# Last chunk of both MLPs in a trunk kernel: from four plain quadrants to the seven products, in an order that completes the first half of the tokens two products early

## The chip, the cores and the metric

The kernel runs on one core of a Trainium2 chip. The metric is the device time of one execution, in microseconds (us); the median of three runs is the time of a kernel. The engines are TensorE (PE, with its weight loads as PEld), VectorE (DVE), ScalarE (ACT), GpSimd (POOL) and SyncE (SP), which here only starts DMAs.

## The reference, cut to what matters

A trunk of two layers works on x, 512 tokens by 1024 features in float32. Layer 0 mixes tokens by latent attention, layer 1 by an mLSTM. After each mixer comes an MLP with squared ReLU, and these two MLPs are what the change touches:

```python
def sqrelu_mlp(h, w1, w2):
    return jnp.square(jax.nn.relu(h @ w1)) @ w2

for i in range(DEPTH):                       # DEPTH = 2
    ...
    x = x + y.astype(x.dtype)                # y: the token mixer
    x = x + sqrelu_mlp(rms_norm(x, norm_ffn[i]), ffn_w1[i], ffn_w2[i])
```

w1 is 1024 by 4096 and w2 is 4096 by 1024.

## The kernel before

**Stages.** The program runs four stages in turn: the attention mixer, MLP 0, the mLSTM mixer, MLP 1. Both MLPs are the same function `ffn` with `last` false or true. The residual x lies in SBUF as eight tiles `xs[t, f]` of 128 tokens by 512 features (t = 0 to 3, f = 0 or 1).

**Numbers.** Every float32 operand is split into a high and a low part. A weight tile of 128x1024 is cast by ACT (`wh`), and DVE subtracts that from the original (`wl<-tw,wh`, or `zw` where the pair lies in a borrowed z tile; a hidden tile gives `hh` and `hl`). A product is then three matmuls: high by high, high by low, low by high. All of the names in the rows are of this kind: `tw` is a raw tile of w2, `wr` another raw weight, `z` a hidden tile, `tp` and `mm` are PSUM banks from two pools (four and three buffers).

**Chunks.** The 4096 hidden features go in NC = 8 chunks of 512. The first matrix is worked through in units ("F", i), i = 0 to 31, 24 matmuls each, four to a chunk. The second is multiplied by Winograd's form of Strassen's seven products, units ("P", c, n): a 2 by 2 block product in seven block products rather than eight. Each unit is 12 matmuls: two token tiles (one PSUM bank each) of six. The table `PROD` gives for n = 0 to 6 the left side, the right side, the chain of banks, and the quadrant (th, f) of x that the bank is added into: 0 A11·b11, chain a, (0,0); 1 S1·t1, chain b, (1,1); 2 S2·t2, a, (0,1); 3 S4·b22, b, (0,1); 4 S3·t3, a, (1,1); 5 A12·b21, c, (0,0); 6 A22·t4, a, (1,0). A chain's two banks gather several products, and after each product two DVE instructions (`y_add`, written y{c}{n} below; in rows `x<-tp,r,x`) add the banks into x. S1 to S4 are sums of hidden blocks, four POOL instructions of 128x256; t1 to t4 are sums of weight blocks, one POOL instruction of 128x1024 each. t2 is written over b11 and t4 over t1.

**The last chunk before.** Chunk 7 is plain: `l_split` splits b11, b21, b12, b22 as they are, and `l_mm` works four quadrants, each of two token tiles of 12 matmuls, 96 in all, without sums. After quadrant (1,0) the transposes of the finished token half stand between the matmuls (`half`).

**What follows.** In MLP 1 `half` is `out`: four PE transposes into an `mm` bank, a copy to a `t` tile of 128x512 by ACT or DVE, and one DMA to the output; there are two `t` tiles. In MLP 0 it is `nxt.half`, which transposes and splits x as the mLSTM's input (`xg`); what is left of it (`nxt.tail`) runs behind the first block of the mLSTM's matmuls.

**Order.** DVE's and PE's instructions of `ffn` are kept in the order of the code (`idve`, `ipe`); ACT's and POOL's in `ffn` and all others are placed by a scheduler. The list `units` sets the order of units; `ahead` splits weights two units early. Around the end of an MLP it is, with Pcn for ("P", c, n): P60 F29 P61 F30 P62 P63 F31 P64 P65 P66, and then the quadrants.

Of the kernel before, what the change touches and what calls it, by code (L numbers as in the profile page):

```python
# [17 lines left out]
F32R = mybir.dt.float32r  # L18
# [43 lines left out]
def trunk(ctx: ExitStack, tc, a, yT, dbg=None):  # L62
# [661 lines left out]
    def ffn(fp, layer, last):  # L724
# [28 lines left out]
        def f_post(ps, i):  # L753

            c, p = i // 4, i % 4 // 2
            plain = c == NC - 1
            if i % 2 == 0:
                zs[c, p] = fp.tile([P, 8, 256], F32, tag="z", bufs=3, name=nm("z"))
            z = zs[c, p]
            t_ = tmp()  # L760
            iact.activation(t_, ps, AF.Relu)
            iact.activation(z[:, 1:3] if i % 2 else z[:, 0:4:3] if plain else z[:, 0:8:7],
                            t_.rearrange("p (h e) -> p h e", h=2), AF.Square)
            if i % 2 == 0:
                return
            hi = fp.tile([P, 7, 256], F32R, tag="hh", bufs=4, name=nm("hh"))
            lo = fp.tile([P, 7, 256], F32R, tag="hl", bufs=4, name=nm("hl"))
            hs[c, p] = hi, lo

            def split(b):  # L770
                iact.copy(hi[:, b], z[:, b])
                idve.tensor_sub(lo[:, b], z[:, b], hi.bitcast(F32)[:, b])

            if plain:
                later.append([s_now[0] + 1, lambda: split(slice(0, 4))])
                return
            ipool.tensor_add(z[:, S1], z[:, A21], z[:, A22])
            ipool.tensor_sub(z[:, S2], z[:, S1], z[:, A11])
            ipool.tensor_sub(z[:, S3], z[:, A11], z[:, A21])
            ipool.tensor_sub(z[:, S4], z[:, A12], z[:, S2])  # L780
            later.append([s_now[0] + 1, lambda: split(slice(0, 3))])
            later.append([s_now[0] + 2, lambda: split(slice(3, 7))])
# [16 lines left out]
                tw[c, n] = b(to)  # L799

        def s_split(c, n):
            ws["P", c, n] = split_w(tw[c, PROD[n][1]], D, iact, idve)

        def s_mm(c, n):
            lhs, _, chain, (th, f) = PROD[n]
            wh, wl = ws.pop(("P", c, n))
            new = n in (0, 1, 5)
            if n < 2:
                bank[chain] = [ps_tp(), ps_tp()]
            for t in range(2):  # L810
                ps = bank["b" if chain == "c" else chain][t]
                for p in range(2):
                    lh, ll = (x[:, lhs, t * P:(t + 1) * P] for x in hs[c, p])
                    rh, rl = (x[:, p * 512:(p + 1) * 512] for x in (wh, wl))
                    skip = not new
                    ipe.matmul(ps, lhsT=lh, rhs=rh, start=new and p == 0, stop=False, skip_group_check=skip)
                    ipe.matmul(ps, lhsT=lh, rhs=rl, start=False, stop=False, skip_group_check=skip)
                    ipe.matmul(ps, lhsT=ll, rhs=rh, start=False, stop=p == 1, skip_group_check=skip)

            def post():  # L820
                for t in range(2):
                    y_add(2 * th + t, f, bank["b" if chain == "c" else chain][t])
# [6 lines left out]
        def l_split(n, roomy):  # L829

            to = None
            if roomy:
                z = fp.tile([P, 2, D], F32R, tag="z", bufs=3, name=nm("zw"))
                to = z[:, 0], z[:, 1]
            ws["L", n] = split_w(tw[NC - 1, n], D, iact, idve, to=to)

        def l_mm(th, f, t, part=slice(0, 12)):
            ps = bank["L", f][t]
            todo = []
            for h in range(2):  # L840
                wh, wl = ws["L", f"b{h + 1}{f + 1}"]
                for p in range(2):
                    lh, ll = (x[:, ((A11, A12), (3, A22))[th][h], t * P:(t + 1) * P] for x in hs[NC - 1, p])
                    rh, rl = (x[:, p * 512:(p + 1) * 512] for x in (wh, wl))
                    todo += [(lh, rh), (lh, rl), (ll, rh)]
            for n in range(12)[part]:
                ipe.matmul(ps, lhsT=todo[n][0], rhs=todo[n][1], start=n == 0, stop=n == 11)
# [28 lines left out]

# [30 lines left out]
        s_sum(0, "t1")  # L907
        s_load(0, ("b21", "b22"))
        s_sum(0, "t3")
        for s_ in range(2, len(units)):  # L910
            u = units[s_]
            if u[0] == "F":
                ps = ps_mm()
                f_mm(ps, u[1])
                ws.pop(u)
            else:
                post = s_mm(u[1], u[2])
            ahead(s_)
            s_now[0] = s_
            while later and later[0][0] <= s_:  # L920
                later.pop(0)[1]()
            if u[0] == "F":
                f_post(ps, u[1])
                if s_ < 5:
                    norm.square(s_ - 1, 0)
                    norm.square(s_ - 1, 1)
                    if s_ == 4:
                        idve.reciprocal(r2, norm.stat())
            else:
                post()  # L930
# [9 lines left out]
                if c == NC - 2 and k > 3:  # L940
                    if k == 4:
                        l_split("b11", False)
                    elif k == 5:
                        l_split("b21", True)
                    else:
                        l_split("b12", True)
# [9 lines left out]
        for n, (th, f) in enumerate(((0, 0), (0, 1), (1, 0), (1, 1))):  # L956
            bank["L", f] = [ps_tp(), ps_tp()]
            for t in range(2):
                if last and n == 3 and t == 1:
                    l_mm(th, f, t, slice(0, 8))  # L960
                    out(4, (2,))
                    l_mm(th, f, t, slice(8, 12))
                else:
                    l_mm(th, f, t)
                if n == 0 and t == 0:
                    l_split("b22", True)
                y_add(2 * th + t, f, bank["L", f][t])
                if n == 2:
                    half(0, ((0, 2), (4, 6))[t])
                if n == 3 and t == 0:  # L970
                    half(1, (0, 2))
                if not last and n < 2:
                    nxt.square(t, f)
                if not last and n == 3:
                    nxt.square(2 + t, 0)
# [8 lines left out]
    def mlstm(lp):  # L984
# [62 lines left out]
        for h in range(MH):  # L1047
# [7 lines left out]
            for t in range(NB):  # L1055
# [216 lines left out]
```

## Time and profile before

| what | before |
|---|---|
| three runs | 1138.22, 1137.02, 1136.86 us; median 1137.02 |
| profiled execution | 1137.65 us; its span, first to last instruction, 1135.8 us |
| mean granted TensorE clock | 0.998 of full speed |
| busy shares | PE 98%, PEld 84%, DVE 73%, ACT 49%, POOL 40% |

The span is the time between the first and the last instruction in the trace; the device time holds 1.85 us more around it. Shares are means over the whole span. The stretch in which the change lies is the last 40 us or so of each MLP: about 548 to 585 us (MLP 0) and 1097 us to the end (MLP 1).

### The profile page before, as it was taken

Reading aid. Unit: us, or ns where it says so; the run is one execution under the profiler, and the core shown is the slowest. Engines: PE = TensorE matmul, PEld = TensorE weight load, DVE = VectorE, ACT = ScalarE, POOL = GpSimd, SP = SyncE. Lnnn points to the kernel's source line nnn. Section 1 sums busy time; section 2 is a strip of 40 time slices with the busy share of each in tenths; the row PEclk is TensorE's granted clock in tenths of the full one; section 3 lists DMA queues with packets and bytes.
Section 4 is the critical chain, followed back from the end, with each engine's and each line's share of the span. In section 5 each row is a group of like instructions: output and inputs, shape, how many; then the busy total and the mean of one; then the engine's idle time right before and its main releaser. Section 6 shows DMA issues by size and latency. Waiting matters only on the chain.

```text
span 1135.8 us, 15650 instructions
## 1 busy us (share of the span) xinstructions
PE 1113.4 (98%) x5802; PEld 949.7 (84%) x5802; DVE 824.1 (73%) x1284; ACT 553.0 (49%) x969; POOL 455.1 (40%) x453
## 2 busy tenths in 40 slices
PE   7899999999999999999999999999999999999998
PEld 7889988888888888888898898888888888888886
DVE  7689997456798788778766465454588779779863
ACT  4468876336544444445455333332655444444451
POOL 6667785207356347335011011010537437436500
PEclk9999999999999999999999999999999999999999
DMA  6301021433432333343203222232333343333212
GB/s 204 115 25 47 20 76 38 134 102 118 130 102 76 119 111 90 96 130 93 76 23 106 78 61 88 75 94 82 140 111 93 93 130 93 93 111 108 60 56 74
DMA packets 32428, 104.27 MB, mean 92 GB/s; under 512 B 3424, under 2 KB 6752, under 8 KB 32352
## 3 DMA queue, kind: packets, MB, share of 16 engines
q1 hardware_dynamic: 32352, 103.27, 29.7%
q8 instruction: 46, 0.75, 0.3%
q14 instruction: 30, 0.25, 0.1%
HBM read 101.16 MB, written 2.10 MB: 91 GB/s over the span
## 4 chain that ended last, share of the span: by engine, by line
PE 93%; DVE 3%; POOL 2%; ACT 1%; issue 1%; DMA 0%; SPq 0%; ACTq 0%; POOLq 0%; DVEq 0%
PE mm L80 39%; PE tp L80 38%; PE mm L174 4%; PE mm L176 4%; PE mm L175 4%; PE po L80 3%; PE tp L176 1%; PE tp L175 1%; PE tp L174 1%; DVE wl L80 1%; ACT t L80 1%; DVE x L80 1%; POOL x L80 0%; POOL scr L80 0%; DMA x<-in_xT 0%
## 5 line engine op out<-in xcount | busy, mean ns | idle before, releaser
L80 PE MATMUL mm<-xg,wh 128*128 128x512 f32 (+1 forms) x1088 | 319.2, 377 | 0.0
L80 POOL TENSOR_TENSOR z<-z 128x256 f32<-128x256 f32 x112 | 129.4, 1175 | 320.4 <-ACT z L80 318.2
L80 PEld LDWEIGHTS mm<-xg,wh 128*128 128x128 f32 x1088 | 200.2, 188 | 37.3
L80 DVE TENSOR_TENSOR wl<-tw,wh 128x1024 fp32r<-128x1024 f32 x100 | 172.7, 1727 | 74.8 <-ACT wh L80 74.8
L80 PE MATMUL mm<-xg,wl 128*128 128x512 f32 (+1 forms) x544 | 206.4, 379 | 0.0
L80 POOL TENSOR_TENSOR tw<-tw,tw 128x1024 f32<-128x1024 f32 x56 | 160.1, 2867 | 34.7 <-issue 29.2
L80 PE MATMUL tp<-wh,hl 128*128 128x512 f32 x408 | 159.0, 390 | 1.3 <-DVE hl L80 1.3
L80 DVE TENSOR_TENSOR wl<-wr,wh 128x1024 fp32r<-128x1024 f32 (+1 forms) x72 | 120.0, 1667 | 55.0 <-ACT wh L80 55.0
L80 DVE SCALAR_TENSOR_TENSOR x<-tp,r,x 128x512 f32<-128x512 f32 (+1 forms) x215 | 149.8, 734 | 13.6 <-PE tp L80 13.5
L80 PE MATMUL tp<-wh,hh 128*128 128x512 f32 x408 | 159.1, 390 | 0.0
L80 PE MATMUL tp<-wl,hh 128*128 128x512 f32 x408 | 158.8, 389 | 0.0
L80 ACT ACTIVATE t<-mm 128x512 f32<-128x512 f32 (+3 forms) x97 | 54.3, 560 | 203.9 <-PE mm L80 194.8
L80 PEld LDWEIGHTS mm<-xg,wl 128*128 128x128 f32 x544 | 102.4, 188 | 22.9 <-DVE wl L80 4.5
L80 ACT CAST wh<-tw 128x1024 fp32r<-128x1024 f32 x100 | 104.7, 1047 | 34.4 <-PE tp L80 26.5
L80 ACT CAST wh<-wr 128x1024 fp32r<-128x1024 f32 (+1 forms) x74 | 78.9, 1067 | 32.1 <-PE tp L80 27.7
L80 PEld LDWEIGHTS tp<-wh,hl 128*128 128x128 f32 x408 | 76.6, 188 | 18.0 <-DVE hl L80 2.1
L80 PEld LDWEIGHTS tp<-wh,hh 128*128 128x128 f32 x408 | 76.6, 188 | 16.5 <-ACT zw L80 0.8
L80 PEld LDWEIGHTS tp<-wl,hh 128*128 128x128 f32 x408 | 76.6, 188 | 15.8
L164 DVE TENSOR_TENSOR wl<-wr,wh 128x1024 fp32r<-128x1024 f32 (+2 forms) x43 | 51.4, 1196 | 44.4 <-ACT wh L160 44.3
L80 ACT CAST hh<-z 128x1024 fp32r<-128x1024 f32 (+1 forms) x60 | 57.0, 949 | 53.4 <-POOL z L80 53.4
L80 DVE TENSOR_TENSOR hl<-z,hh 128x1024 fp32r<-128x1024 f32 (+1 forms) x60 | 82.9, 1382 | 0.0
L160 ACT CAST wh<-wr 128x1024 fp32r<-128x1024 f32 (+2 forms) x43 | 42.8, 995 | 77.1 <-PE mm L175 27.9
(275 smaller groups left out, 2065.3 us busy)
## 6 DMA issues: line engine op xcount, KB each, us to landing
wr<-in_w SPq DMA_DIRECT2D x64, 512.0 KB, 3.6
tw<-in_w SPq DMA_DIRECT2D x64, 512.0 KB, 3.6
wr<-in_w_qkv SPq DMA_DIRECT2D x8, 640.0 KB, 4.1
wr<-in_w_oa SPq DMA_DIRECT2D x8, 512.0 KB, 3.7
wr<-in_w_mo SPq DMA_DIRECT2D x8, 512.0 KB, 3.5
wr<-in_w_ob SPq DMA_DIRECT2D x8, 512.0 KB, 3.5
wr<-in_w_v SPq DMA_DIRECT2D x6, 512.0 KB, 3.8
wr<-in_w_z SPq DMA_DIRECT2D x8, 336.0 KB, 4.5
```

The lines of the kernel that those rows point to most:

```text
L80: return lambda *args, **kw: tc.keep_in_program_order(f(*args, **kw)) if self.on else f(*args, **kw)
L160: act.copy(hi[:, :n], raw[:, :n])
L164: dve.tensor_sub(lo[:, :n], raw[:, :n], hi[:, :n].bitcast(F32))
L174: pe.matmul(out, lhsT=lh, rhs=rh, start=start, stop=False)
L175: pe.matmul(out, lhsT=lh, rhs=rl, start=False, stop=False)
L176: pe.matmul(out, lhsT=ll, rhs=rh, start=False, stop=stop)
```

## The change

Chunk 7 of both MLPs goes by the seven products, 84 matmuls, in the order 0, 5, 1, 2, 3, 4, 6. The sums S1 to S4 and t1 to t4 are now made for chunk 7 as for the others. Product 5 (chain c) gets two `mm` banks of its own, where in other chunks it uses chain b's. Products 4 and 6 are worked by single token tiles (`ts`), with the transposes of the first token half between them, since quadrants (0,0) and (0,1) are complete after product 3. Their weights' splits go to z tiles. In MLP 1 the eight output copies are in the order out(0), out(2), out(4), out(6) for the first half and 4, 6 and the two pieces of 0 for the second; in MLP 0 parts 0 and 2 of the second half go into `nxt.tail`.

```diff
@@ f_post
-            plain = c == NC - 1
...
-            if plain:
-                later.append([s_now[0] + 1, lambda: split(slice(0, 4))])
-                return
             ipool.tensor_add(z[:, S1], z[:, A21], z[:, A22])
...
@@ s_split
+            to = None
+            if c == NC - 1 and n in (4, 6):
+                z = fp.tile([P, 2, D], F32R, tag="z", bufs=3, name=nm("zw"))
+                to = z[:, 0], z[:, 1]
+            ws["P", c, n] = split_w(tw[c, PROD[n][1]], D, iact, idve, to=to)
@@ s_mm
-        def s_mm(c, n):
+        def s_mm(c, n, ts=(0, 1)):
...
+            if ts[0] == 0:
+                if n < 2:
+                    bank[chain] = [ps_tp(), ps_tp()]
+                elif n == 5:
+                    bank["c"] = bank["b"] if c < NC - 1 else [ps_mm(), ps_mm()]
...
@@ units
-        for c in range(NC - 1):
-            for k in range(7):
+        for c in range(NC):
+            for k in range(7) if c < NC - 1 else (0, 5, 1, 2, 3):
                 units.append(("P", c, k))
...
+        units += [("P", NC - 1, 4), ("P", NC - 1, 6)]
@@ loop
-                elif k == 5 and c < NC - 2:
+                if k == (5 if c < NC - 2 else 4):
                     s_sum(c + 1, "t1")
-                elif k == 6 and c < NC - 2:
+                elif k == (6 if c < NC - 2 else 5):
                     s_sum(c + 1, "t3")
@@ tail
+        s_mm(C, 4, (0,))()
+        half(0, (0,))
+        s_mm(C, 4, (1,))()
+        half(0, (2, 4, 6))
+        s_mm(C, 6, (0,))()
+        half(1, (4, 6))
         if last:
-            out(4, (3,))
+            post = s_mm(C, 6, (1,))
+            out(0, (2,))
+            post()
         else:
-            nxt.tail = [lambda m=m: nxt.half(1, m, ps_tp) for m in (4, 6)]
+            s_mm(C, 6, (1,))()
...
+        if last:
+            out(0, (3,))
+        else:
+            nxt.tail = [lambda m=m: nxt.half(1, m, ps_tp) for m in (0, 2)]
```

What this does to the order on POOL at the end of MLP 1 is shown first; these are POOL's last sums before the change, hidden sums of chunk 6 and then t1 to t4 of chunk 6 (the digits behind a name only number buffers).

```order
L80 TENSOR_TENSOR z_9949<-z_9949 128x256 x4
L80 TENSOR_TENSOR tw_10055<-tw_9918,tw_9916 128x1024
L80 TENSOR_TENSOR tw_9916<-tw_9993,tw_10055 128x1024
L80 TENSOR_TENSOR tw_9918<-tw_9993,tw_9918 128x1024
L80 TENSOR_TENSOR tw_10055<-tw_9991,tw_9916 128x1024
```

After the change two blocks of hidden sums and four weight sums of chunk 7 stand behind those; they are POOL's last.

```order
L80 TENSOR_TENSOR z_10111<-z_10111 128x256 x4
L80 TENSOR_TENSOR z_10250<-z_10250 128x256 x4
L80 TENSOR_TENSOR tw_10356<-tw_10274,tw_10272 128x1024
L80 TENSOR_TENSOR tw_10272<-tw_10354,tw_10356 128x1024
L80 TENSOR_TENSOR tw_10274<-tw_10354,tw_10274 128x1024
L80 TENSOR_TENSOR tw_10356<-tw_10352,tw_10272 128x1024
```

So POOL, which had nothing in this place, has eight hidden sums (four of them before F31's end) and four weight sums here.

DVE at the same place, from F31's end in MLP 1, before the change: the splits of P66's weights and of the plain hidden tile, then pairs of adds y64, y65, y66 (SCALAR_TENSOR_TENSOR) with the splits of b11, b21, b12 and b22 between them.

```order
L80 TENSOR_TENSOR wl_10313<-tw_10055,wh_10312 128x1024
L80 TENSOR_TENSOR hl_10299<-z_10222,hh_10298 128x1024
L80 SCALAR_TENSOR_TENSOR x_3185<-tp_10114,r_1502_8002,x_3185 128x512
L80 SCALAR_TENSOR_TENSOR x_3189<-tp_10115,r_1502_8002,x_3189 128x512
L80 TENSOR_TENSOR wl_10325<-tw_10244,wh_10324 128x1024
L80 SCALAR_TENSOR_TENSOR x_3175<-tp_10169,r_1502_8002,x_3175 128x512
L80 SCALAR_TENSOR_TENSOR x_3179<-tp_10170,r_1502_8002,x_3179 128x512
L80 TENSOR_TENSOR zw_10342<-tw_10320,zw_10342 128x1024
L80 SCALAR_TENSOR_TENSOR x_3183<-tp_10114,r_1502_8002,x_3183 128x512
L80 SCALAR_TENSOR_TENSOR x_3187<-tp_10115,r_1502_8002,x_3187 128x512
L80 TENSOR_TENSOR zw_10359<-tw_10246,zw_10359 128x1024
L80 TENSOR_TENSOR zw_10376<-tw_10322,zw_10376 128x1024
```

After it, DVE has here the split of P66's weights, two splits of the hidden tile (768 elements, then the 1024 of S1 to S4), and between y64, y65, y66 the splits for P70 (b11), P75 (b21) and P71 (t1, `tw_10356`, a POOL result).

```order
L80 TENSOR_TENSOR wl_10345<-tw_10077,wh_10344 128x1024
L80 TENSOR_TENSOR hl_10327<-z_10250,hh_10326 128x768
L80 SCALAR_TENSOR_TENSOR x_3185<-tp_10136,r_1508_8024,x_3185 128x512
L80 SCALAR_TENSOR_TENSOR x_3189<-tp_10137,r_1508_8024,x_3189 128x512
L80 TENSOR_TENSOR wl_10371<-tw_10272,wh_10370 128x1024
L80 TENSOR_TENSOR hl_10327<-z_10250,hh_10326 128x1024
L80 SCALAR_TENSOR_TENSOR x_3175<-tp_10195,r_1508_8024,x_3175 128x512
L80 SCALAR_TENSOR_TENSOR x_3179<-tp_10196,r_1508_8024,x_3179 128x512
L80 TENSOR_TENSOR wl_10393<-tw_10352,wh_10392 128x1024
L80 SCALAR_TENSOR_TENSOR x_3183<-tp_10136,r_1508_8024,x_3183 128x512
L80 SCALAR_TENSOR_TENSOR x_3187<-tp_10137,r_1508_8024,x_3187 128x512
L80 TENSOR_TENSOR wl_10413<-tw_10356,wh_10412 128x1024
```

The instructions are of the same kinds as before, with one more split in front and with inputs that POOL makes in the same stretch; then come five more pairs of adds and four more splits.

DVE in the tail of MLP 0 after the change, from the split of P74's weights on: `wl` at L164 are splits for the mLSTM's first weights (1056 wide) and the next (1024 wide), `x_3177` and `x_3181` with `tp_5782` and `tp_5783` are y72 and with `tp_5823` and `tp_5824` y73, `x_3185` is y74's first half, and `xg` the low parts of `half(0, 0)`.

```order
L80 TENSOR_TENSOR zw_5855<-tw_5658,zw_5855 128x1024
L80 SCALAR_TENSOR_TENSOR x_3177<-tp_5782,r_737_3408,x_3177 128x512
L164 TENSOR_TENSOR wl_6010<-wr_6007,wh_6009 128x1056
L80 SCALAR_TENSOR_TENSOR x_3181<-tp_5783,r_737_3408,x_3181 128x512
L80 TENSOR_TENSOR zw_5872<-tw_5740,zw_5872 128x1024
L164 TENSOR_TENSOR wl_6016<-wr_6013,wh_6015 128x1056
L80 SCALAR_TENSOR_TENSOR x_3177<-tp_5823,r_737_3408,x_3177 128x512
L80 SCALAR_TENSOR_TENSOR x_3181<-tp_5824,r_737_3408,x_3181 128x512
L164 TENSOR_TENSOR wl_6219<-wr_6216,wh_6218 128x1024
L80 SCALAR_TENSOR_TENSOR x_3185<-tp_5782,r_737_3408,x_3185 128x512
L80 SCALAR_TENSOR_TENSOR xg_5885<-mm_5905,cst,xg_5877 128x256
L80 SCALAR_TENSOR_TENSOR xg_5886<-mm_5905,cst,xg_5878 128x256
```

The adds of y73, which finish x for `half(0, 4)` and `half(0, 6)`, stand behind three splits, and the low parts of `half(0, 0)` behind one more and an add.

## Rows read from the trace of the kernel before

**Rows 1.** The page: busy time by engine; the ending chain's share by engine.

```profile
PE 1113.4 (98%) x5802; PEld 949.7 (84%) x5802; DVE 824.1 (73%) x1284; ACT 553.0 (49%) x969; POOL 455.1 (40%) x453
...
PE 93%; DVE 3%; POOL 2%; ACT 1%; issue 1%; DMA 0%; SPq 0%; ACTq 0%; POOLq 0%; DVEq 0%
```

**Rows 2.** The chain that ended last, MLP 1's end: start us, us, what.

```profile
1058.78 2.72 PE tp L80 x12
...
1097.11 22.04 PE tp L80 x96
...
1132.06 0.58 ACT t L80
```

**Rows 3.** Busy time by windows: length, PE, PEld, DVE, ACT, POOL (instructions), granted clock, DMA share, GB/s.

```profile
1097.11:1118.88 21.77, 21.77 (x96) 17.71 (x96) 13.77 (x16) 6.91 (x8) 0.00 (x0) 1.00 0.00 0
```

**Rows 4.** Timeline of DVE, 1095 to 1136: start, us, instruction.

```profile
1100.52 1.22 DVE L80 TENSOR_TENSOR hl<-z,hh 128x1024 fp32r<-128x1024 f32 x1
1101.65 1.40 DVE L80 SCALAR_TENSOR_TENSOR x<-tp,r,x 128x512 f32<-128x512 f32 x2
1102.97 1.22 DVE L80 TENSOR_TENSOR wl<-tw,wh 128x1024 fp32r<-128x1024 f32 x1
```

**Rows 5.** Timeline of POOL from 1050 to the end: all it has.

```profile
1060.16 4.65 POOL L80 TENSOR_TENSOR z<-z 128x256 f32<-128x256 f32 x4 [16.92 <-ACT z L80]
1064.77 2.40 POOL L80 TENSOR_TENSOR tw<-tw,tw 128x1024 f32<-128x1024 f32 x1
1068.39 6.60 POOL L80 TENSOR_TENSOR tw<-tw,tw 128x1024 f32<-128x1024 f32 x2 [1.22 <-issue]
1076.21 2.41 POOL L80 TENSOR_TENSOR tw<-tw,tw 128x1024 f32<-128x1024 f32 x1 [1.21 <-issue]
```

**Rows 6.** Timeline of DVE beside those POOL rows, from 1061.

```profile
1061.05 1.74 DVE L80 TENSOR_TENSOR wl<-tw,wh 128x1024 fp32r<-128x1024 f32 x1 [4.75 <-ACT wh L80]
1062.72 1.49 DVE L80 TENSOR_TENSOR hl<-z,hh 128x768 fp32r<-128x768 f32 x1
1064.13 1.40 DVE L80 SCALAR_TENSOR_TENSOR x<-tp,r,x 128x512 f32<-128x512 f32 x2
1065.45 2.81 DVE L80 TENSOR_TENSOR wl<-tw,wh 128x1024 fp32r<-128x1024 f32 x1
...
1069.32 3.41 DVE L80 TENSOR_TENSOR wl<-wr,wh 128x1024 fp32r<-128x1024 f32 x1
```

**Rows 7.** Timelines of ACT and DVE: output copies from `mm` to `t` (MLP 1).

```profile
1119.63 0.59 ACT L80 COPY t<-mm 128x512 f32<-128x512 f32 x1 [15.54 <-PE mm L80]
1124.74 0.59 ACT L80 COPY t<-mm 128x512 f32<-128x512 f32 x1 [4.53 <-DMA out_yT<-t]
1127.58 0.59 ACT L80 COPY t<-mm 128x512 f32<-128x512 f32 x1 [2.25 <-DMA out_yT<-t]
...
1125.40 0.69 DVE L80 COPY t<-mm 128x512 f32<-128x512 f32 x1 [1.85 <-DMA out_yT<-t]
...
1128.39 0.69 DVE L80 COPY t<-mm 128x512 f32<-128x512 f32 x1 [1.22 <-DMA out_yT<-t]
```

**Rows 8.** The chain that ended last, at the end of MLP 0.

```profile
548.55 22.04 PE tp L80 x96
570.59 0.87 PE mm L80 x8
...
581.43 2.90 PE mm L80 x24
```

**Rows 9.** Timeline of DVE in the tail of MLP 0.

```profile
573.97 1.23 DVE L164 TENSOR_TENSOR wl<-wr,wh 128x1024 fp32r<-128x1024 f32 x1 [0.37 <-ACT wh L160]
...
575.77 1.65 DVE L80 SCALAR_TENSOR_TENSOR xg<-mm,cst,xg 128x256 fp32r<-128x256 f32 x4
```

**Rows 10.** Windows in the attention mixer, columns as in rows 3.

```profile
60.00:66.00 6.00, 3.90 (x28) 3.27 (x27) 4.95 (x19) 3.42 (x8) 4.95 (x7) 1.00 0.06 10
66.00:70.00 4.00, 4.00 (x23) 3.91 (x21) 3.29 (x13) 1.74 (x6) 3.26 (x6) 0.57 0.41 154
```

More of the change, by code (lines that the diff above doesn't have):

```diff
@@ L761, in f_post @@
             iact.activation(t_, ps, AF.Relu)
-            iact.activation(z[:, 1:3] if i % 2 else z[:, 0:4:3] if plain else z[:, 0:8:7],
+            iact.activation(z[:, 1:3] if i % 2 else z[:, 0:8:7],
                             t_.rearrange("p (h e) -> p h e", h=2), AF.Square)
@@ L801, in s_split @@
         def s_split(c, n):
-            ws["P", c, n] = split_w(tw[c, PROD[n][1]], D, iact, idve)
-        def s_mm(c, n):
+            to = None
[4 more added lines that the diff above has]
+        def s_mm(c, n, ts=(0, 1)):
             lhs, _, chain, (th, f) = PROD[n]
-            wh, wl = ws.pop(("P", c, n))
+            wh, wl = ws["P", c, n]
             new = n in (0, 1, 5)
[L808 to L811, printed above, removed]
+            if ts[0] == 0:
[3 more added lines that the diff above has]
+                    bank["c"] = bank["b"] if c < NC - 1 else [ps_mm(), ps_mm()]
+            banks = list(bank[chain])
+            for t in ts:
+                ps = banks[t]
                 for p in range(2):
@@ L820, in post @@
             def post():
-                for t in range(2):
-                    y_add(2 * th + t, f, bank["b" if chain == "c" else chain][t])
+                for t in ts:
+                    y_add(2 * th + t, f, banks[t])
             return post
@@ L826, in y_add @@
             idve.scalar_tensor_tensor(xs[t, f], ps, r2[:, t:t + 1], xs[t, f], op0=mult, op1=add)
[L829 to L847, printed above, removed]
         def out(m, ts):
@@ L866, in ffn @@
         n = 5
-        for c in range(NC - 1):
-            for k in range(7):
+        for c in range(NC):
+            for k in range(7) if c < NC - 1 else (0, 5, 1, 2, 3):
                 units.append(("P", c, k))
-                if k in ((0, 2, 4, 5) if c < NC - 2 else (0, 1, 3)):
+                if n < 4 * NC and k in ((0, 2, 4, 5) if c < NC - 2 else (0, 1, 3)):
                     units.append(("F", n))
                     n += 1
-        at = {u: s_ for s_, u in enumerate(units)}
+        units += [("P", NC - 1, 4), ("P", NC - 1, 6)]
         def ahead(s_):
@@ L909, in ffn @@
         s_sum(0, "t3")
-        for s_ in range(2, len(units)):
+        for s_ in range(2, len(units) - 2):
             u = units[s_]
@@ L931, in ffn @@
                 c, k = u[1], u[2]
+                if c == NC - 1:
+                    continue
                 if k == 2:
@@ L935, in ffn @@
                     s_load(c + 1, ("b21", "b22"))
-                elif k == 5 and c < NC - 2:
+                if k == (5 if c < NC - 2 else 4):
                     s_sum(c + 1, "t1")
-                elif k == 6 and c < NC - 2:
+                elif k == (6 if c < NC - 2 else 5):
                     s_sum(c + 1, "t3")
[L940 to L946, printed above, removed]
         nxt = None if last else Norm(C_NM + KD)
@@ L955, in half @@
                     nxt.half(th, m)
-        for n, (th, f) in enumerate(((0, 0), (0, 1), (1, 0), (1, 1))):
-            bank["L", f] = [ps_tp(), ps_tp()]
+        if not last:
             for t in range(2):
[L959 to L975, printed above, removed]
+                nxt.square(t, 0)
+        C = NC - 1
+        s_mm(C, 4, (0,))()
[4 more added lines that the diff above has]
+        half(1, (4, 6))
         if last:
-            out(4, (3,))
-        else:
-            nxt.tail = [lambda m=m: nxt.half(1, m, ps_tp) for m in (4, 6)]
+            post = s_mm(C, 6, (1,))
+            out(0, (2,))
+            post()
+        else:
+            s_mm(C, 6, (1,))()
+            for t in range(2):
+                nxt.square(t, 1)
+                nxt.square(2 + t, 1)
+        if last:
+            out(0, (3,))
+        else:
+            nxt.tail = [lambda m=m: nxt.half(1, m, ps_tp) for m in (0, 2)]
             norms.append(nxt)
@@ L1067, in mlstm @@
                     for i in range(2):
-                        norm.square(2 + i, 1)
+                        norm.square(2 + i, 0)
                     iact.on = False
```

## The prediction

> **What bounds the kernel now.** First the page's busy shares and the shares of the chain that ended last: PE is busy 98% of the span and holds 93% of the chain [rows 1]. So matmuls taken away are worth their time, as long as PE has no wait in their place. Then the chain at the end of MLP 1: 12 matmuls of a product take 2.72 us, 0.2267 each, and the last stretch, P64 P65 P66 and the first 60 matmuls of the plain chunk, is one piece of 96 matmuls in 22.04 us from 1097.11 [rows 2]; 96 x 0.2267 is 21.76, so PE loses only 0.28 us there. Then the other engines in that stretch [rows 3]: DVE is busy 13.77 of 21.77 us, POOL does nothing. The change gives work to both. Last, the tails. After MLP 1 the output copies on ACT each wait for a DMA out of a `t` tile [rows 7], so there PE is not the limit; after MLP 0 PE runs on without a gap into the mLSTM, whose first matmuls start at 581.43 [rows 8].
>
> **What is removed.** 96 matmuls become 84: 12 x 0.2267 = 2.72 us of PE per MLP, 5.44 in both. Eight quadrant tiles of adds become 14 and four weight splits become seven, all on DVE; POOL gets eight hidden sums and four weight sums per MLP.
>
> **What DVE has to do per product.** A split costs 1.13 us start to start (1101.65 less 1100.52), a pair of adds 1.32 (1102.97 less 1101.65) [rows 4]: 2.45 us for each product of 2.72. Before, units F stood between products (24 matmuls for one split) and, in the last chunk, a quadrant of 5.44 us had one split and one pair. After F31 the eight products P64 to P73 run back to back, and 0.27 us of slack per product is all that DVE has.
>
> **What POOL does to DVE.** One stretch in the trace of before has the same start: after F27, which ended at 1058.78 [rows 2], POOL makes four hidden sums and t1 to t4 [rows 5], beside the same DVE instructions (split, hidden split of 768, two adds, split) [rows 6]. There a split that meets a POOL sum doesn't take 1.22 us but ends about 1.1 us after the sum does: t1 ends at 1064.77 + 2.40 = 1067.17, the split from 1065.45 at 1068.26, 2.81 us; t2 and t3 start with the row at 1068.39, and a split from 1069.32 takes 3.41. The adds, which read a PSUM bank, keep their 1.40 a pair in this company [rows 6]. In that stretch F28 and F29 (5.44 us of PE each) took up the delay. After the change no F is left behind F31.
>
> **The walk, MLP 1.** I move that stretch by 38.33 us (1097.11 less 1058.78) [rows 2] and follow it. Without waits P64, P65, P66, P70, P75, P71, P72, P73 would start 2.72 apart from 1097.11, and P74 at 1118.87.
> - The adds y64 start at 1064.13 + 38.33 = 1102.46 [rows 6]; the first is done 0.7 later, and P66, which goes on in that bank, starts at 1103.3 instead of 1102.55.
> - The split for P70 is the 2.81 us one and ends at 1106.6 [rows 6]; the hidden split (S1 to S4) follows to 1107.7, and y65's first add ends at 1108.4. P70 takes that bank: 1108.5 instead of 1105.27, 3.2 late.
> - t2 (from 1106.7, two sums in 6.60 us [rows 5]) ends at about 1110.0, and the split for P75 1.1 later, 1111.1; P75 starts on time after P70, 1111.2. y66 takes DVE to 1112.4. t3 ends at 1113.3, the split for P71 at 1114.4: P71 starts there, not at 1113.9.
> - t4 is written over t1, which the split for P71 has just read: 1114.5 to 1116.9 by 2.41 us [rows 5]. The split for P72 stands against it and ends at 1118.0; P72 starts then, 0.9 after P71's end.
> - y75, the split for P73, and y71's first add (1.32 + 1.13 + 0.66) end at 1121.2; P73 continues in y71's bank, 0.6 late. P74 then starts at about 1124.0.
>
> This is 5.1 us behind the plan. Before had lost 0.28; 2.72 is saved: P74 and what follows lie about 2.1 us later than the corresponding work of before. Bounds: nothing, where sums and splits don't meet (POOL quicker or earlier, or PE's order tolerant of it), and, at the top, each of four weight sums paid whole, 4 x 2.4 = 9.6 us [rows 5]. I take 5.1, since the row after F27 is the same order on both engines.
>
> **The tail, MLP 1.** The ring of two `t` tiles has a cycle of 2.84 us on ACT (1127.58 less 1124.74) and 2.99 on DVE (1128.39 less 1125.40); the first cycle of before was slow, 5.11 (1124.74 less 1119.63) [rows 7]. After: P74's first tile ends at 1125.4, four transposes at 0.109 each (0.87 for 8 [rows 8]), first copy at about 1126.0; P74's second tile, then the copy of out(2) into the second `t` tile at 1127.8. That tile's four copies are 2.99 apart: 1127.8, 1130.8, 1133.8, 1136.8. The last copy of before began at 1132.06 [rows 2] and the span ended at 1135.8, 3.74 later: 1136.8 + 3.74 = 1140.5, **+4.7 us**. If a slow first cycle comes again, 2.3 more (5.11 less 2.84). Even with no wait before P74 (1118.87), the second tile's ring gives 1122.7 + 3 x 2.99 + 3.74 = 1135.4, 0.4 less than before: the two matmul tiles saved in MLP 1 are mostly given back in the ring.
>
> **The tail, MLP 0.** The same walk, moved by 548.55 less 1097.11 [rows 2, 8], puts P74 at 575.4. From there PE has four tiles of 1.36 us, four parts of transposes and two more, 0.44 each (6 x 0.44 = 2.62): 8.06 us, 583.5. Two waits come in. DVE does the splits for P74 and P76 between the adds of P72, and the mLSTM's two splits of 1056 stand ahead of y73; by the splits' 1.2 us ([rows 9] has one of 1.23) DVE is through with y73 at about 580.5, and `half(0, 4)`, ready on PE at 579.0, waits 1.5. Then a third split (1.14), y74's first add (0.66) and the low parts of `half(0, 0)` (0.4 each, 1.65 for 4 [rows 9]) stand between that and the release of the third `mm` bank, at 583.1, for which `half(0, 6)` waits 2.1 us, since its predecessor is done at 581.0. The mLSTM's first matmul: 583.5 + 1.5 + 2.1 = 587.1 instead of 581.43 [rows 8], **+5.7 us**. With no wait there it would be +2.1, and with none in the whole stretch 570.31 + 8.06 = 578.4, -3.1. What comes after is PE's own [rows 1], so it is carried to the end.
>
> **A rule against it.** In the mixer PE was busy 3.90 of 6 us, and in the 4 us behind that the granted clock was 0.57, most of it on the lower level [rows 10]; in this stretch PE would be busy about 21.8 of 26.9 us, 0.81, and has been at 1.00 [rows 3]. The same loss again would be (1 - 0.57) x 4 = 1.7 us per MLP, partly hidden as DVE sets the pace; the sum leaves it out. The Trainium skill ("TensorE: Matmul & The Clock Gate", What's actually happening) says that the clock is gated by default and that activity releases it, which speaks for such a loss; the trace agrees for the mixer, not yet here.
>
> **Sum.** 1137.65 (the profiled execution) + 5.7 + 4.7 = 1148.1; it lies 0.6 above the median of the runs (1137.02), so the median should be **1147.5**. A change of 0.2%, 2.3 us, is about what a measurement can tell from none.
>
> **Rivals.**
> - Saved matmuls are saved (faster). DVE has slack enough, POOL's sums end before the splits start, and PE meets no wait: MLP 0 -3.1, MLP 1 -0.4, at the most -5.44 for both if the ring has no slack either way: 1131.6 to 1133.5. It decides if the waits before P74 are below about 1 us in each MLP. For it: 0.27 us of slack per product, and POOL could do its sums earlier. Against: hidden sums can't start before F31 ends, and the rows after F27 show the waits. Chance 0.08.
> - Half of it (same). Splits don't meet sums as often, P74 is some 2.5 us late, and the tail of MLP 0 waits once: MLP 0 about -3.1 + 2.5 + 1.5 = +0.9, MLP 1 about -0.4 + 2.5 less 0.28 = +1.8; with somewhat less, +0 to +2.3: 1137 to 1139.3. Chance 0.07.
> - Partly: the walk right to P74, but the tail of MLP 0 orders DVE so that y73 isn't behind the mLSTM's splits (+2.1 to +3.6 there): 1140 to 1145. Chance 0.17.
> - The forecast, 1145 to 1151, 0.55.
> - Worse: a slow first ring cycle (+2.3), half clock (+1.7 to 3.4), or a split that waits for a second sum: 1151 to 1156. Chance 0.13.
>
> So faster 0.08, same 0.07, slower 0.85. The range 1139.5 to 1153 leaves out the first two cases and the upper part of the last. The likeliest case's own is 1145 to 1151.
>
> **What would show it.** Step by step: matmuls 24 fewer; POOL with eight sums between 1097 and 1117; DVE splits of 2 to 3.4 us there; P70 about 3 us behind P66's end; P74 some 27 us after F31's end; in MLP 0 waits of PE before the third and fourth transposes; the mLSTM's start at 587; the second `t` tile's copies 3 us apart as the last thing. The prediction is wrong if splits stay at 1.2 us, if PE's stretch after F31 is below 23.5 us, or if the scheduler's order of the mLSTM's splits on DVE doesn't bind as the rows of the order say.

## The result: 1151.37 us, 1.3% slower

Four runs of the changed kernel give 1150.77 to 1152.72 us, median 1151.37; the kernel before, beside them on the same chip, 1136.43 to 1138.22, median 1136.94. The ratio is 1.0127, 95% interval 1.0115 to 1.0139: 14.4 us slower. The forecast was 1147.5 with a range of 1139.5 to 1153. The profiled execution took 1151.77 us, span 1150.0.

The page after, to be read against [rows 1]:

```profile
PE 1112.7 (97%) x5778; PEld 946.1 (82%) x5778; DVE 853.1 (74%) x1306; ACT 562.8 (49%) x979; POOL 497.0 (43%) x477
```

PE has its 24 matmuls less. The time lost lies in two places. First the end of MLP 0, F31 having ended at 547.96; the timeline of DVE (start us, us, instruction) has the splits for P70, P75, P71 and P72:

```profile
554.62 2.78 DVE L80 TENSOR_TENSOR wl<-tw,wh 128x1024 fp32r<-128x1024 f32 x1
...
559.78 2.07 DVE L80 TENSOR_TENSOR wl<-tw,wh 128x1024 fp32r<-128x1024 f32 x1
...
563.10 2.10 DVE L80 TENSOR_TENSOR wl<-tw,wh 128x1024 fp32r<-128x1024 f32 x1
...
566.43 2.40 DVE L80 TENSOR_TENSOR wl<-tw,wh 128x1024 fp32r<-128x1024 f32 x1
```

Beside them the timeline of POOL has:

```profile
549.33 4.63 POOL L80 TENSOR_TENSOR z<-z 128x256 f32<-128x256 f32 x4 [14.20 <-ACT z L80]
553.92 2.40 POOL L80 TENSOR_TENSOR tw<-tw,tw 128x1024 f32<-128x1024 f32 x1
557.54 6.58 POOL L80 TENSOR_TENSOR tw<-tw,tw 128x1024 f32<-128x1024 f32 x2 [1.22 <-issue]
565.33 2.43 POOL L80 TENSOR_TENSOR tw<-tw,tw 128x1024 f32<-128x1024 f32 x1 [1.21 <-issue]
```

Each of the four weight sums has one of these splits behind it: t1 ends at 556.32, the split from 554.62 at 557.40, and so on, 2.1 to 2.8 us where the same split takes 1.2 in [rows 4]. The chain that ended last then shows, from P73 on (start us, us, what):

```profile
572.09 4.37 PE tp L80 x18
576.46 0.45 PE mm L80 x4
...
577.28 1.24 DVE wl L164
...
582.57 1.07 PE mm L80 x4
583.64 2.53 PE tp L80 x6
586.17 0.87 PE mm L80 x8
587.04 1.38 PE tp L80 x6
588.42 2.90 PE mm L80 x24
```

P73 and P74's first tile are 18 matmuls, four transposes follow, and then the chain leaves PE for DVE, which is at the mLSTM's splits (L164). The last row is the mLSTM's start: 588.42, where [rows 8] have 581.43, 7.0 us later. Counted from F31's end it is 40.5 us, where before had 32.9 (581.43 less 548.55): 7.6 more, since F31 ended 0.6 us earlier in this execution than in the one before the change. P76's first tile (583.64) takes 2.53 us for six matmuls, its second (587.04) 1.38. The waits of PE in this stretch, by who ended them (total, times, longest):

```profile
PE tp L80 <- DVE x L80: 3.4, 3, 2.2
PE mm L80 <- DVE xg L80: 2.1, 1, 2.1
PE mm L80 <- DVE x L80: 0.8, 2, 0.5
PE tp L80 <- DVE wl L80: 0.6, 1, 0.6
```

The first row is P66, P70 and P73, each before a bank that an add has still to read (0.8, 2.2 and 0.4 us), and the last is P72 before its split. The other two belong to the tail: 0.8 us before `half(0, 4)`, for y73, and 2.1 before `half(0, 6)`, for the third `mm` bank, which the low parts of `half(0, 0)` (`xg`) have to release.

Second the end of MLP 1 in the same chain, F31 having ended at 1103.73:

```profile
1115.11 4.56 PE tp L80 x12
1119.67 2.72 PE mm L80 x12
1122.39 9.76 PE tp L80 x42
...
1135.39 4.50 DMA out_yT<-t
...
1140.73 2.27 DMA out_yT<-t
...
1143.84 2.23 DMA out_yT<-t
...
1146.25 0.59 ACT t L80
```

P70 takes 4.56 us for 12 matmuls, P75 behind it 2.72. From 1135 on the chain is one `t` tile going out three times. Behind F31's end there are 46.27 us to the end of the span (1150.0), where before had 38.69 (1135.8 less 1097.11): 7.6 more. The two stretches together are 15.2 us longer, the span 14.2: the missing 1.0 is F31 of MLP 0, 0.6 us earlier, and the stretch from the mLSTM's start to F31 of MLP 1, 0.4 us shorter (515.3 for 515.7). What shortened these isn't shown.

The granted clock in windows (columns as in [rows 3]):

```profile
1112.00:1118.00 6.00, 3.82 (x12) 2.77 (x11) 6.00 (x6) 1.04 (x1) 4.78 (x3) 0.76 0.00 0
...
580.00:584.00 4.00, 1.88 (x9) 1.57 (x10) 4.00 (x8) 1.16 (x3) 0.00 (x0) 0.82 0.65 232
584.00:588.00 4.00, 4.00 (x19) 3.24 (x18) 2.67 (x7) 1.87 (x6) 0.00 (x0) 0.75 0.02 8
```

In both places the clock was on the lower of its levels, 1.2 GHz, for a part of the stretch, each time behind waits of PE: matmuls start 0.43 us apart instead of 0.2267.

### The profile page after: what moved, and what is told of

It is laid out like the page before. It is cut to its first block, busy times and chain, and to the rows that moved or that the text cites. A ratio compares the mean times of both kernels' runs of the same rounds, so it can differ in the third digit from the quotient of the medians.

```text
span 1150.0 us, 15677 instructions
## 1 busy us (share of the span) xinstructions
PE 1112.7 (97%) x5778; PEld 946.1 (82%) x5778; DVE 853.1 (74%) x1306; ACT 562.8 (49%) x979; POOL 497.0 (43%) x477
## 4 chain that ended last, share of the span: by engine, by line
PE 89%; DVE 5%; issue 2%; POOL 2%; ACT 2%; DMA 1%; SPq 0%; ACTq 0%; DVEq 0%; POOLq 0%
PE mm L80 39%; PE tp L80 34%; PE mm L174 4%; PE mm L176 4%; PE mm L175 4%; PE po L80 3%; DVE x L80 1%; DVE wl L80 1%; DMA out_yT<-t 1%; DVE hl L80 1%; PE tp L176 1%; PE tp L175 1%; PE tp L174 1%; ACT t L80 1%; POOL x L80 0%
## 5 line engine op out<-in xcount | busy, mean ns | idle before, releaser
L80 POOL TENSOR_TENSOR z<-z 128x256 f32<-128x256 f32 x128 | 148.0, 1176 | 350.8 <-ACT z L80 348.3
L80 DVE TENSOR_TENSOR wl<-tw,wh 128x1024 fp32r<-128x1024 f32 x108 | 194.1, 1797 | 74.8 <-ACT wh L80 74.8
L80 POOL TENSOR_TENSOR tw<-tw,tw 128x1024 f32<-128x1024 f32 x64 | 182.6, 2861 | 39.4 <-issue 34.1
L80 PE MATMUL tp<-wh,hh 128*128 128x512 f32 x424 | 166.2, 392 | 6.4 <-DVE x L80 6.4
L80 PE MATMUL tp<-wh,hl 128*128 128x512 f32 x424 | 165.7, 391 | 0.9 <-DVE hl L80 0.9
L80 PE MATMUL tp<-wl,hh 128*128 128x512 f32 x424 | 165.8, 391 | 0.6 <-DVE wl L80 0.6
L80 DVE SCALAR_TENSOR_TENSOR x<-tp,r,x 128x512 f32<-128x512 f32 (+1 forms) x223 | 154.9, 732 | 0.9 <-PE tp L80 0.8
L80 ACT CAST wh<-tw 128x1024 fp32r<-128x1024 f32 x108 | 113.1, 1048 | 49.6 <-PE tp L80 37.2
L80 ACT CAST hh<-z 128x768 fp32r<-128x768 f32 x64 | 60.3, 942 | 61.8 <-POOL z L80 61.7
L80 DVE TENSOR_TENSOR hl<-z,hh 128x768 fp32r<-128x768 f32 x64 | 86.7, 1354 | 0.0
L164 DVE TENSOR_TENSOR wl<-wr,wh 128x1024 fp32r<-128x1024 f32 (+2 forms) x43 | 51.4, 1198 | 44.2 <-ACT wh L160 44.1
```

The lines of the kernel that those rows point to most:

```text
L80: return lambda *args, **kw: tc.keep_in_program_order(f(*args, **kw)) if self.on else f(*args, **kw)
L164: dve.tensor_sub(lo[:, :n], raw[:, :n], hi[:, :n].bitcast(F32))
```

## The experiments

The theory after the result: the loss has three causes. (1) Behind F31, POOL's sums hold up DVE's splits, and DVE has no slack to catch up, so PE waits until P74. (2) In MLP 0's tail, y73 and the release of a bank stand behind the mLSTM's splits on DVE. (3) In MLP 1's tail, two `t` tiles set the pace. Each of the runs below takes one away, moves it, or puts it in where it wasn't.

**The change in MLP 0 alone** (MLP 1's `ffn` is that of the kernel before):

```diff
-        ffn(pool, 1, True)
+        ffn_last(pool, 1, True)        # the function before the change
```

> The change in MLP 0 alone, MLP 1's last chunk plain as before. My theory (each MLP pays for itself: waits of PE on DVE up to P74, then MLP 0's waits in its tail): the mLSTM's first matmul came 7.0 us later in the changed kernel (588.42 against 581.43), so 1136.9 + 6.6 to 7.0 = 1143.5 to 1144. Rival (the loss is mainly MLP 1's ring of output tiles, and MLP 0's delay is taken up in the mLSTM): 1137 to 1139.

Measured: 1144.22 us, ratio to before 1.0063 (1.0050 to 1.0075). Half of the loss is MLP 0's, and nothing is taken up in the mLSTM. The rival falls.

**Weight sums by loads:**

```diff
-                ipool.tensor_sub(b("t1"), b("b12"), b("b11"))
+                if c == NC - 1:
+                    nc.sync.dma_start(b("t1"), a["w2"][layer, c, 0])
+                else:
+                    ipool.tensor_sub(b("t1"), b("b12"), b("b11"))
...
-                ipool.tensor_sub(b(to), b(x), b(y))
+                if c == NC - 1:
+                    nc.sync.dma_start(b(to), a["w2"][layer, c, 1])
+                else:
+                    ipool.tensor_sub(b(to), b(x), b(y))
```

> Chunk 7's four weight sums on POOL are replaced by loads of raw tiles into the same places (so t1 to t4 hold other numbers than the sums); POOL keeps the hidden sums, everything else stays. Theory (DVE's splits are held up by POOL's weight sums): splits of 1.2 us, P74 about 23.4 us behind F31's end instead of 26.9, in both MLPs: 1151.4 - 7 = about 1144.5. Rival (DVE has too much work there by itself, POOL or not): P74 stays at 26 to 27 us, 1150 to 1152.

Measured: 1142.55, ratio 1.0048 (1.0036 to 1.0061): 8.8 us less than the change. DVE's timeline has the splits for P70 and P75 in MLP 0 so, and the chain that ended last has P70 and P71 to P74 in MLP 1:

```profile
554.38 1.21 DVE L80 TENSOR_TENSOR wl<-tw,wh 128x1024 fp32r<-128x1024 f32 x1
...
557.97 1.21 DVE L80 TENSOR_TENSOR wl<-tw,wh 128x1024 fp32r<-128x1024 f32 x1
```

```profile
1107.21 3.01 PE tp L80 x12
...
1112.94 9.52 PE tp L80 x42
```

F31 ended at 1097.41, so P70 starts 9.8 us behind it (changed kernel 11.4). P74, inside the last row, starts at 1120.93 in the timeline of PE, 23.5 behind it (26.9). DVE's own work there is unchanged; the rival, that it is too much by itself, explains only what is left of the delay, 1.8 us over eight products of 2.72. P74 accounts for 3.4 us per MLP; most of the other 2 us come from MLP 0's tail, where P76's first tile takes 1.39 us here for 2.53 in the changed kernel.

**Sixteen output tiles:**

```diff
-            o = tmp()
+            o = up.tile([P, T], F32, tag="xg", bufs=2 * KD, name=nm("o"))
```

> MLP 1's outputs are copied into the sixteen tiles of the normalised x, which are free by then, instead of two t tiles. Theory (the ring of two tiles sets MLP 1's end): the copies follow PE, the last one at about P74 + 8.7 us, 1139.3 on the changed kernel's axis instead of 1146.25, so 7 us less: about 1144.5. Rival (the output transfers themselves are late, and more tiles only queue them): 1149 to 1151.5.

Measured: 1146.51, ratio 1.0080 (1.0066 to 1.0094), 4.9 us less than the change and 2.0 above the theory's number. The last copy in the chain that ended last:

```profile
1140.96 0.59 ACT o L80
```

F31 ended at 1104.15: the copy comes 36.8 us behind it, where the changed kernel has 42.5 and I had expected 35.6. The ring was the bound; behind it comes PE, whose last four transposes wait for y76.

**Transposes later in MLP 0:**

```diff
-        half(0, (2, 4, 6))
+        half(0, (2, 4, 6) if last else (2,))
         s_mm(C, 6, (0,))()
-        half(1, (4, 6))
+        half(1, (4, 6)) if last else half(0, (4, 6))
```

(the second half's parts 4 and 6 then follow P76's second tile).

> MLP 0 only: the transposes of parts 4 and 6 of the first token half move behind P76's first tile, those of the second half behind P76's second. Theory (PE waited 3.5 us in MLP 0's tail for y73 behind the mLSTM's splits on DVE, and lost 1.5 more at the lower clock after it): 3.5 to 5 us less, 1146.5 to 1148. Rival (the waits come back at the next place, before the mLSTM's first matmuls): 1150 to 1152.

Measured: 1150.85, ratio 1.0123 (1.0108 to 1.0139), 0.5 less, as the rival said. The chain that ended last shows where the wait went:

```profile
580.33 1.13 DVE wl L164
581.46 0.67 DVE x L80
...
582.27 1.61 PE tp L80 x6
```

P76's first tile now waits for y74, which stands behind the third of the mLSTM's splits. In this execution, the quickest of the four at 1150.10, the mLSTM still starts 38.5 us behind F31's end instead of 40.5, so PE's order mends a part of what is late on DVE, but the medians show almost nothing of it.

**The same sums, earlier** (b22's tile and t1 to t3 are allocated behind P63, t2 in a z tile):

```diff
+                if c == NC - 2:
+                    if k == 1:
+                        s_load(c + 1, ("b11", "b12"))
+                    elif k == 3:
+                        s_sum(c + 1, "t1")
+                        s_load(c + 1, ("b22",))
+                        s_load(c + 1, ("b21",))
+                        s_sum(c + 1, "t3")
+                        s_sum(c + 1, "t2")
+                    continue
```

> The same seven products and the same sums, but chunk 7's raw weights are loaded earlier and in another order, t1, t3 and t2 are summed on POOL before F31 ends (t2 into a free z tile), t4 over t2 late. Theory (splits held up by POOL's weight sums): as with the loaded tiles, splits of 1.2 us behind F31, P74 at about 23.4 us after F31's end: 1142 to 1144. Rival (the loaded tiles helped because POOL's instructions were gone altogether, and moved sums cost the same in another place): 1149 to 1152.

Measured: 1149.33, ratio 1.0107 (1.0094 to 1.0121). A miss, of the edit rather than of the theory, as POOL's timeline in MLP 0 shows:

```profile
547.90 2.41 POOL L80 TENSOR_TENSOR tw<-tw,tw 128x1024 f32<-128x1024 f32 x1 [7.14 <-DMA tw<-in_w]
...
552.62 5.57 POOL L80 TENSOR_TENSOR z<-z 128x256 f32<-128x256 f32 x4
```

b22's load had to wait for a tile, two sums came just when F31 ended, and F31's hidden sums began at 552.62, 4.2 us behind F31's end, where the changed kernel has 1.4. The second form, b22 loaded ahead of t1's allocation and t3 in the z tile's other half:

```diff
-                        s_sum(c + 1, "t1")
                         s_load(c + 1, ("b22",))
-                        s_load(c + 1, ("b21",))
                         s_sum(c + 1, "t3")
+                        s_sum(c + 1, "t1")
+                        s_load(c + 1, ("b21",))
                         s_sum(c + 1, "t2")
```

> Of that only the place of the sums: t3, t1 and t2 of chunk 7 on POOL before F31's hidden sums, t4 late; the rest as in the changed kernel. Theory: F31's hidden sums are not put off this time (P66 at most 0.8 us late), P74 at about 23.5 us after F31's end in both MLPs, and no lower clock in the stretch: 1142.5 to 1145, as with loaded tiles. Rival (the sums cost the same wherever they lie): 1148 to 1151.

Measured: 1143.72, ratio 1.0057 (1.0043 to 1.0070), 7.7 less than the change, with every sum still made. The timelines of DVE (splits for P70 and P73) and POOL (t4) in MLP 0:

```profile
553.76 1.21 DVE L80 TENSOR_TENSOR wl<-tw,wh 128x1024 fp32r<-128x1024 f32 x1
...
564.75 2.33 DVE L80 TENSOR_TENSOR wl<-tw,wh 128x1024 fp32r<-128x1024 f32 x1
```

```profile
563.59 2.41 POOL L80 TENSOR_TENSOR t<-tw,t 128x1024 f32<-128x1024 f32 x1 [9.79 <-DVE wl L80]
```

Only the split beside t4, the one weight sum left behind P66, is held up. P70 and P71 to P74 in the chain that ended last, MLP 1:

```profile
1109.03 2.97 PE tp L80 x12
...
1114.72 9.60 PE tp L80 x42
```

F31 ended at 1099.61: P70 starts 9.4 us behind it and P74 (1122.80 in the timeline of PE) 23.2. So it isn't how much POOL sums, but beside what.

**The mLSTM's first splits on POOL:**

```diff
-            ws = [load_w(src[c], 4 * nv) for c in range(2)]
+            ws = [split_w(load_raw(src[c], 4 * nv), 4 * nv, dve=nc.vector if h else nc.gpsimd) for c in range(2)]
```

(and the same for the first `w_mq`).

> The subtractions of the mLSTM's first three weight splits go from DVE to POOL, which has nothing else in MLP 0's tail; all else as in the changed kernel. Theory (in MLP 0's tail PE waits for adds that stand behind those splits on DVE): the 3.5 us of waits go, and with them the lower clock behind them: 3.5 to 5 us less, 1146.5 to 1148. Rival (the adds are late by DVE's backlog from before, or POOL's slower splits are late for the mLSTM): 1150 to 1153.

Measured: 1148.98, ratio 1.0104 (1.0089 to 1.0120), 2.4 less than the change. It lies between the two expectations. In the chain that ended last, `half(0, 6)` and the mLSTM's start:

```profile
581.51 0.63 PE mm L80 x4
...
585.79 2.90 PE mm L80 x24
```

F31 ended at 548.28, the mLSTM starts 37.5 us behind it instead of 40.5. `half(0, 4)` waits no more, but `half(0, 6)` (581.51) still waits 1.0 us for its bank, and P74's first tile waits 0.6 for y72, which stands behind a split of 2.40 us beside one of POOL's new ones.

**Product 5 before product 0:**

```diff
-            for k in range(7) if c < NC - 1 else (0, 5, 1, 2, 3):
+            for k in range(7) if c < NC - 1 else (5, 0, 1, 2, 3):
```

> Only the order: product 5 of chunk 7 (in the two mm banks) before product 0, so that no product has to wait at once for the bank that y65 reads. Theory (DVE has no time left from F31 to P74, and every wait of PE there is its backlog): the wait moves to a later product, P74 stays at 26 to 27 us after F31's end, 1150 to 1152. Rival (the 2.3 us wait of P70 for its bank is a loss of its own): about 2.3 us less in each MLP, 1146 to 1147.5.

Measured: 1155.24, ratio 1.0155 (1.0141 to 1.0169). No gain, as the theory has it, but 3.9 us worse than the change, which neither said. In the profiled execution, at 1152.43 the quickest of the four, P74 comes 29.0 and 28.7 us behind F31's end in the two MLPs, not 26 to 27, and the trace shows one cause. On POOL t3 now stands right behind t1, since t2, written over b11, has to wait for b11's later split; beside t3 is the second hidden split (timeline of DVE, MLP 1):

```profile
1112.69 3.42 DVE L80 TENSOR_TENSOR hl<-z,hh 128x1024 fp32r<-128x1024 f32 x1
```

It takes 1.21 us in the changed kernel. In MLP 0 the mLSTM starts no later for it (40.4 us behind F31's end). Why the other three executions take 3 us more stays open.

**Sums in the plain chunk.** The reverse of the second run: the kernel before, with POOL additions behind F31 that nothing reads.

```diff
                 later.append([s_now[0] + 1, lambda: split(slice(0, 4))])
+                for _ in range(3 if i == 4 * NC - 1 else 0):
+                    ipool.tensor_add(z[:, 4:8], z[:, 0:4], z[:, 0:4])
                 return
```

> The kernel before, plain last chunk, with three POOL additions of 128x1024 put behind F31 in both MLPs; they write a part of the hidden tile that nothing reads, so the result is the same. Theory (a split can't run beside such an addition, whatever the product): DVE's two splits behind F31 wait for one addition each, P66 starts 3 to 4 us late by y64, the next bank 4 to 4.6 by y65, and with plain quadrants nothing catches up: 4 us per MLP, about 1143 to 1146. Rival (POOL's sums cost time only because the seven products fill DVE): 1136.5 to 1138.

Measured: 1145.34, ratio 1.0075 (1.0062 to 1.0087): 8.2 us. The timelines of DVE and of POOL in MLP 0:

```profile
550.14 2.08 DVE L80 TENSOR_TENSOR wl<-tw,wh 128x1024 fp32r<-128x1024 f32 x1 [4.75 <-ACT wh L80]
552.14 2.91 DVE L80 TENSOR_TENSOR hl<-z,hh 128x1024 fp32r<-128x1024 f32 x1
554.98 1.40 DVE L80 SCALAR_TENSOR_TENSOR x<-tp,r,x 128x512 f32<-128x512 f32 x2
```

```profile
549.25 7.56 POOL L80 TENSOR_TENSOR z<-z 128x1024 f32<-128x1024 f32 x3 [19.91 <-ACT z L80]
```

The splits are held up, the adds keep their 1.40 a pair: the exclusion needs no seven products. The Trainium skill ("SBUF — State Buffer", Who interferes with whom) states it: a DVE instruction with two SBUF inputs contends with a GpSimd instruction that reads SBUF; one with at most one SBUF input, outside the modes that take both of DVE's ports, doesn't. The traces of all of these runs agree: no add into x takes more than 0.75 us, beside POOL or not, while splits beside POOL's sums take up to 3.42. The chain that ended last has, from P66 to the first transposes:

```profile
555.86 18.20 PE tp L80 x72
```

The size came out as forecast, 4.1 us in MLP 0 (37.0 from F31's end to the mLSTM, 32.9 before), but not its make-up: P66 is 2.5 us late, not 3 to 4, and these 72 matmuls take 1.6 us more than in the kernel before, as seven of them start 0.43 us apart behind that wait.

**All mended.** A first form joined the early sums (first edit), the POOL splits, the sixteen tiles, and the second hidden split one unit later:

```diff
-            later.append([s_now[0] + 2, lambda: split(slice(3, 7))])
+            later.append([s_now[0] + (2 if i < 4 * NC - 1 else 3), lambda: split(slice(3, 7))])
```

> The early sums, the mLSTM's first splits on POOL and the ring of sixteen output tiles together, and the second hidden split of F31 one unit later. Theory (three independent causes): P74 22 to 23 us after F31's end in both MLPs, no waits in MLP 0's tail, MLP 1 ends 36 to 37.5 us after F31's end: 1131.5 to 1134.5, below the kernel before (1137). Rival (the causes hide one another, DVE has no slack and the waits come back elsewhere): 1137 to 1141.

Measured: 1139.27, ratio 1.0021 (1.0012 to 1.0030), as the rival said: F31's hidden sums were late again, and in MLP 0 DVE's last three splits, now beside t4 and the mLSTM's splits on POOL, took 2.2 to 2.3 us each. The second form takes the second edit of the sums, and puts those POOL splits behind the last split of chunk 7:

```diff
         half(0, (0,))
+        if not last:
+            nv = DV + 2 * MH
+            nxt.w0 = [split_w(load_raw(a["w_v0"][c], 4 * nv), 4 * nv, iact, ipool) for c in range(2)]
         s_mm(C, 4, (1,))()
-        half(0, (2, 4, 6))
+        if last:
+            half(0, (2, 4, 6))
+        else:
+            half(0, (2, 4))
+            nxt.half(0, 6, ps_tp)
```

> All causes mended together, second form: b22 is loaded into the place that comes free first, t3, t1 and t2 are summed before F31's hidden sums (t2 and t3 into a free z tile), the second hidden split one unit later, the mLSTM's first two splits on POOL behind the split for P76, half(0, 6) in a tp bank, and the ring of sixteen output tiles. Theory (POOL sums beside DVE's splits, the mLSTM's splits ahead of y73, the two output tiles are all of the loss): P74 22.5 to 23.5 us after F31's end, the mLSTM 1 to 2 us and MLP 1's end 1 to 2 us earlier than in the kernel before: 1132.5 to 1135. Rival (DVE has no slack in this order, whatever POOL does): 1137 to 1140, as with the first form.

Measured: 1135.07, ratio 0.9982 (0.9973 to 0.9991): 2.0 us below the kernel before, just above the theory's 1132.5 to 1135. One wait was left before `half(0, 6)`, 1.3 us between two starts of PE, and it is ACT's: the new casts stand between its copies. With those three added lines ahead of P74's first tile:

> As the second form of all mendings, but the casts and POOL subtractions of the mLSTM's first two splits come before P74 in the program, so that ACT makes them ahead of the high parts of half(0, 0) to half(0, 6). Theory (the 1.3 us wait that was left before half(0, 6) is ACT's: the casts stand between the copies): that wait goes, 1 to 1.5 us less than the second form, 1133.5 to 1134.2. Rival (the POOL splits then block the split for P76 on DVE, and the wait moves there): 1134.8 to 1136.

Measured: 1134.34, ratio 0.9977 (0.9968 to 0.9986), between the two expectations; the step between the two forms, 0.7 us, is within their intervals, but the wait is gone from the trace. The rows of the chain that ended last which answer to the three causes, the mLSTM's start and MLP 1's end:

```profile
579.95 2.90 PE mm L80 x24
```

```profile
1115.80 4.37 PE tp L80 x18
...
1128.55 0.58 ACT o L80
```

F31 ended at 548.2 and 1095.3: the mLSTM starts 31.8 us behind it (before 32.9), P74 (1118.64 in the timeline of PE) 23.3 (changed kernel 26.9), the last copy 33.3 (before 34.95). The kernel is 2.8 us below the one before, where 5.44 were taken from PE. No run puts the mendings of the tails into the kernel before, so that the 2.8 us are the seven products' alone is not shown; the kernel before leaves them little to mend, since PE runs without a gap into the mLSTM there [rows 8] and its last output copy waits for PE.

## Why the prediction came out as it did

Sign and walk were right. After F31's end, in us:

| start of | forecast | MLP 0 | MLP 1 |
|---|---|---|---|
| P66 | 6.2 | 6.2 | 6.2 |
| P70 | 11.4 | 11.4 | 11.4 |
| P75 | 14.1 | 14.2 | 15.8 |
| P73 | 24.1 | 24.1 | 24.1 |
| P74 | 26.9 | 27.0 | 26.9 |

Moving the stretch after F27 onto the new order gave the delay to 0.1 us; that the cause is POOL beside DVE, which the walk took from two rows, is shown by three runs: sums away (-8.8), sums moved (-7.7), sums put into the plain chunk (+8.2). The column of MLP 1 has one late step, P75, and none after it: P70 ran at the lower clock there, 4.56 us, and P74 came no later, since DVE was what PE waited for.

**MLP 0's tail** was forecast at +5.7; behind F31's end it is 7.6. The waits are those named and of the size named: 0.8 us of idle for y73 and 2.1 for the third bank put `half(0, 6)` off by 3.6 us (forecast 1.5 and 2.1). Left out was the lower clock behind them: the four transposes of `half(0, 6)` take 1.07 us for 0.44, P76's first tile 2.53 for 1.36, together 1.8.

**MLP 1's tail** was forecast at +4.7; behind F31's end it is 7.6. Left out was the slow first cycle of the ring: one tile's copies start at 1134.68, 1140.01 and 1143.12, the first cycle 5.33 us where I put 2.99. That is 2.3 of the missing 2.9 us. One reading was wrong on the way: not every output copy of the kernel before waits for a DMA. The last one, in its timeline of ACT, waits for PE, so MLP 1's end hung on PE there and hangs on the ring now:

```profile
1132.06 0.58 ACT L80 COPY t<-mm 128x512 f32<-128x512 f32 x1 [1.06 <-PE mm L80]
```

Both terms stood in the prediction, as the case "Worse" with a chance of 0.13, and each had its row, [rows 10] and the 5.11 of [rows 7]. The measured 1151.37 lies in that case, inside the stated range but just above the 1145 to 1151 of the likeliest one. What was mis-sized is the sum: it took the undisturbed value for two effects that had been seen in the only rows there were. With its own prices, 1.7 us for the clock in one MLP and 2.3 for the ring, it would have given 1151.5. That this comes so near is in part luck: the tails are 4.8 us over their forecast, and 1.0 came back in stretches that the prediction doesn't speak of. The clock's price was also meant for the stretch up to P74, in either MLP; there it cost nothing in time, and it was paid in MLP 0's tail alone. Of the signs one doesn't fit the walk that it stands behind: P70 "about 3 us behind P66's end" is 2.5 by the walk (1108.5 less 1103.3 and 2.72) and was 2.2.

The rival of saved matmuls failed where the prediction said it would be decided: P74 was over 5 us late in each MLP. "Half of it", with P74 2.5 us late, fell with it; "Partly" fell in MLP 0's tail, where both waits came. The saving isn't lost for good, as the mended kernel shows: it is 2.8 us below the kernel before once POOL's sums, the next stage's splits and the ring are out of DVE's and the output's way.

## What to carry to other kernels

Before work is taken from an engine that is 98% busy, add up what the engine that feeds it has to do per unit of the shorter work; at 2.45 of 2.72 us there is nothing to pay for a disturbance, and each one moves into the bound. An engine that was idle beside a stretch may have been what let it run: adding work to it is not free, so look for a place in the trace where the two already meet and move that stretch onto the new order. A disturbance in the only row that shows an effect belongs into the sum, not into the tail of the range.

## What was not expected of the hardware

- At the ends of the MLPs, the last output transposes left out, these traces have 21 gaps of 2.4 to 3 us between PE's starts. Behind 14 of them six to eight matmuls started about 0.43 us apart instead of 0.2267 (P70 4.56 us, P76's first tile 2.53). Not always, and not always at once: in the changed kernel's MLP 0 P70 waits the same 2.56 us between two starts and runs at the full clock, and so does P76 behind a gap of 3.35 us in the run with the transposes later.
- POOL pays too: t2 and t3 back to back beside splits took 6.58 us, t1 and t4 2.40 to 2.43 each.
- The first output transfer from the ring of two tiles took 3.7 to 4.6 us in all seven traces that have it in their chain (4.50 here), the later ones 2.2 to 2.3. What slows the first stays open; with the ring of sixteen no output transfer stands in the chain before the last copy.
